# Attention scores whose low-part product uses 64 or 128 rows of the array, on one Trainium2 core

## The chip, the cores and the metric

The kernel runs on one core of a Trainium2 chip. The metric is the device time of one execution in microseconds (us); less is better. Engines are named as in the profile: PE is TensorE (matrix products), PEld its weight loads, DVE is VectorE, ACT is ScalarE, POOL is GpSimd, SP is the queue from which most transfers are issued.

## What is computed

One layer of a hybrid block: an input projection, a token mixer with two groups of eight heads (a matrix memory and a differential attention), an output projection and a gated feed-forward part. Batch 1, 512 latent and 256 context tokens, model width 2048. The change sits in the differential attention, which has two components of 64 channels per head:

```
s = jnp.einsum('bqhcd,bkhcd->bhcqk', qblk, k32) * scale
pr = jax.nn.softmax(s, axis=-1)
pd = pr[:, :, 0] - lam * pr[:, :, 1]
return jnp.einsum('bhqk,bkhe->bqhe', pd, v32)
```

Queries are the 512 latent tokens in blocks of 128, keys all 768 tokens. The scalar `lam` comes from four learned vectors of 64 numbers.

## The kernel before, in words

Matrix products run in a rounded 32-bit type. To keep accuracy, each operand is split into a high part (the rounded value, cast on ACT) and a low part (the rest, subtracted on DVE), and products of the parts are summed in PSUM. `load_w` (line 100) does this for every weight chunk of 128 x 512: `whi` on ACT (line 128), `wlo` on DVE (line 129). A projection (`proj`, line 433) multiplies the weights with 512 latent columns (tile `mm`, three products per contraction tile, `mm3`) and, for some outputs, with 256 context columns (tile `cx`).

**Startup.** `setup` loads the constant columns (`cols`, 522 wide, the last 256 of them the four vectors of `lam`) and tables; `startup` loads the 16 tiles `xT` of the input, takes their square sums, and computes the modulation (`mod`, from the chunks `mraw`) and the first projections.

**Attention.** From `attn_setup` on, TensorE runs in program order (`pin`). The projections of the heads go through, and after each short run of products `tick` (line 81) advances one of two queues of generators by one stage: even ticks those of the matrix memory (`mlstm_rest`), odd ticks those of the differential attention (`diff_rest`, line 763). So between two stages of `diff_rest` lie two runs of projection products and a stage of the other queue. The order on the other engines is a scheduler's, except that an engine runs its own list strictly in turn.

**A score.** `diff_q` (line 732) turns the queries of a head by the rotary tables and makes, per component, the tile `qa`: the high part of the 64 channels, twice over the 128 partitions; and one tile `ql` with the low parts of both components, 64 partitions each (line 744). `diff_k` makes per component `kb`: the high part of the keys on 64 partitions and the low part on the other 64. `score(t, c)` (line 769) then computes, for a query block t and a component c, 768 columns in two pieces of 512 and 256. Each piece is two products into the same PSUM columns: `qa` with all 128 rows of `kb` (high times high plus high times low), then `ql` with the 64 rows of the high keys:

```
for ks in (slice(0, 512), slice(512, TA)):
    self.mm(ps[:, ks], hd.qa[c][:, ts], hd.kb[c][:, ks], start=True, stop=False)
    self.mm(ps[:, ks], hd.ql[cs, ts], hd.kb[c][cs, ks], start=False, stop=True)
```

After the products DVE takes the row maximum (line 780, `mx<-sc`), scales it (line 781), and ACT takes the exponential (line 783, `p<-sc,mx`), which frees the PSUM tile `sc`. The pool of `sc` (`ps_big`) has one buffer, so the next score's products wait for that exponential. The stages of `diff_rest` are: score (0,0), transposed values (`vtp`), score (0,1), then for t = 1 to 3 score (t,0), `ptr` (transposes `pt`), score (t,1), `pv` (product `do`). Eight scores per head and eight heads make 64 scores.

Of the kernel before, what the change touches and what calls it, by code (L numbers as in the profile page):

```python
# [6 lines left out]
F32 = mybir.dt.float32  # L7
F32R = mybir.dt.float32r
AF = mybir.ActivationFunctionType
ALU = mybir.AluOpType  # L10
# [4 lines left out]
P = 128  # L15
# [17 lines left out]

# contraction groups of the output projection: the last heads come last
MIXG = [[0, 1, 2, 3], [8, 9, 10, 11], [4, 5, 12, 13], [6, 7, 14, 15]]
# [23 lines left out]
class Prog:  # L59
# [13 lines left out]
    def pe(self, ins):  # L73
        """in the pinned part TensorE runs in program order"""
        if self.pin:
            self.tc.keep_in_program_order(ins)
        return ins

    # one tick after every short run of projection products: the attention of earlier
    # heads goes between them, a stage at a time  # L80
    def tick(self):
# [18 lines left out]
    def load_w(self, src, n, act=False):  # L100
        """src [128, n] in DRAM -> get(column, width) -> (hi, lo)"""
        his, los = [], []
# [33 lines left out]

    # ---------------------------------------------------------------- setup
    def setup(self, ctx):
# [12 lines left out]
        self.dram = e(tc.tile_pool(name="scr", bufs=1, space=DRAM))  # L151
        self.cols = self.p_c.tile([P, NCOLS], F32, name="cols")
        self.tabs = self.p_c.tile([P, NTABS], F32, name="tabs")
        nc.sync.dma_start(self.cols, I["cols"])
        nc.sync.dma_start(self.tabs, I["tabs"])
# [13 lines left out]
    def rstd(self, dst, ss, n, scale):  # L169
        """dst = (ss*scale + eps) ** -0.5 for [128, n]"""  # L170
        nc = self.nc
        nc.vector.tensor_scalar(dst, ss, scale, EPS, ALU.mult, ALU.add)
        nc.gpsimd.tensor_tensor(dst, dst, self.mhalf[:, :n], ALU.pow)

    # ---------------------------------------------------------------- input norm statistics
    def rms_bcast(self, xs, w, name):
        """xs: 16 T-layout tiles [128, w]; returns rstd broadcast over partitions [128, w]"""
        nc = self.nc
# [25 lines left out]
    def mod_a(self, kt):  # L204
        """shift and scale columns of input channel tile kt, for latents and context"""
        nc, I = self.nc, self.I
# [27 lines left out]

    # ---------------------------------------------------------------- late modulation rows
    def modb_steps(self):
        """generator: one weight chunk per step; order ga1, sh2, sc2, ga2"""
        nc, I = self.nc, self.I
# [20 lines left out]
    def modb_cols(self, q, cc, acc):  # L259
        """columns of one of ga1 * g_post_mix, sh2, (1 + sc2) * g_pre_ffn, ga2 * g_post_ffn"""  # L260
        nc = self.nc
# [18 lines left out]

    # ---------------------------------------------------------------- combined input projection
    def phase_in(self):
# [7 lines left out]
        self.mcol = pc.tile([P, 64], F32, name="mcol")  # L290
        # lambda of the differential attention
        lam = self.C("lam").rearrange("p (a b) -> p a b", b=64)
        lt = self.slot("lt")[:, :128].rearrange("p (a b) -> p a b", b=64)
# [67 lines left out]
    def startup(self):  # L361
        nc, I = self.nc, self.I
        # silu of the conditioning vectors
        self.csil = self.p_st.tile([P, KT, 32], F32, name="csil", bufs=1)
# [86 lines left out]

    # ---------------------------------------------------------------- gates of the matrix memory
    def attn_setup(self):
# [22 lines left out]
    def gates(self):  # L476
# [4 lines left out]
        if True:  # L481
# [5 lines left out]
            for dst, r in ((I_, 0), (F_, 64)):  # L487
# [3 lines left out]
                nc.vector.tensor_copy(dst[32:40, TL:TA], gc[r + 32:r + 40, :])  # L491
            # log sigmoid
            nc.scalar.activation(L_, F_, AF.Abs)
            nc.scalar.activation(L_, L_, AF.Exp, scale=-1.0)
            nc.scalar.activation(L_, L_, AF.Ln, bias=1.0)
            nc.vector.scalar_tensor_tensor(F_, F_, 0.0, L_, ALU.min, ALU.subtract)
            # cumulative sums within chunks
            nc.vector.memset(L_, 1.0)
# [5 lines left out]
            nc.vector.tensor_tensor_scan(b_[32:40, ::-1], L_[32:40, ::-1], F_[32:40, ::-1], 0.0, ALU.mult, ALU.add)  # L504
            # running maxima carried over chunks
            nc.vector.tensor_tensor(I_, I_, b_, ALU.subtract)
# [31 lines left out]
            nc.scalar.activation(b_, b_, AF.Exp, scale=-1.0)  # L538
            # rows to be read back on all partitions
            self.row_d = self.dram.tile([2, 2, NH, TL], F32, name="row_d")  # L540
# [9 lines left out]
            for _ in range(9):  # L550
                yield
            # columns
            pa = self.p_at1
# [11 lines left out]

    # ---------------------------------------------------------------- matrix memory heads
    def conv3(self, dst, src, w, n):
# [29 lines left out]
    def tr6(self, src, name):  # L597
        """six 128 x 128 blocks of src [128, 768] transposed; two PSUM views [128, n, 128]"""
        out = []
        for a, n in ((0, 4), (4, 2)):  # L600
            ps = self.ps_sm.tile([P, 512], F32, tag="sm", name=name)
            for j in range(n):
                self.tr(ps[:, j * P:(j + 1) * P], src[:, (a + j) * P:(a + j + 1) * P], self.ident)
            out.append((a, n, ps[:, :n * P].rearrange("p (c d) -> p c d", d=P)))
        return out
# [18 lines left out]
    def mlstm_rest(self, hd, h):  # L624
# [9 lines left out]
        yield  # L634
        # weights within chunks, queries weighted for the carried states
        for d in range(2):
# [7 lines left out]
            nc.gpsimd.tensor_tensor(wrow[d], q, wrow[d], ALU.mult)  # L644
        # keys in natural layout, weighted for the state updates
        parts = self.tr6(k, "kt")
# [13 lines left out]
        yield  # L660
        # scores, shared by both directions
        pss = self.ps_sm.tile([P, 512], F32, tag="sm", name="s")
# [5 lines left out]
        yield  # L668
        # states before each latent chunk
        C = [self.p_cst.tile([P, 4, 129], F32, tag="cst", name="cst") for _ in range(2)]  # L670
# [51 lines left out]

    # ---------------------------------------------------------------- differential attention heads
    def rope(self, dst, src):
# [7 lines left out]
    def diff_q(self, hd, h):  # L732
        nc = self.nc
        q = self.acc.pop(DQ + h)
        self.rope(q, q)
        # per component the high part twice over the partitions, and the low parts
        hd.qa = [self.slot("qa", F32R) for _ in range(2)]
        hd.ql = self.slot("ql", F32R)
        for c in range(2):
            cs = slice(64 * c, 64 * c + 64)  # L740
            os = slice(64 - 64 * c, 128 - 64 * c)
            nc.scalar.copy(hd.qa[c][cs, :], q[cs, :])
            nc.scalar.copy(hd.qa[c][os, :], q[cs, :])
            nc.vector.tensor_tensor(hd.ql[cs, :], q[cs, :], hd.qa[c][cs, :].bitcast(F32), ALU.subtract)

    def diff_k(self, hd, h, psl, psc):
# [4 lines left out]
        self.rope(k[:, TC:TA], k[:, TC:TA])  # L751
        # per component high and low parts stacked over the partitions
        hd.kb = [self.p_a3.tile([P, 774], F32R, tag="a3", name="kb") for _ in range(2)]
# [9 lines left out]
    def diff_rest(self, hd, h):  # L763
        nc = self.nc
        on = self.slot("on")
        ss = self.p_s.tile([P, 4], F32, tag="oss", name="oss")
        st = {}

        def score(t, c):
# [3 lines left out]
            pr, z, mx = st[t]  # L773
            cs = slice(64 * c, 64 * c + 64)
            ts = slice(t * P, (t + 1) * P)
            ps = self.ps_big.tile([P, 1024], F32, tag="big", name="sc")
            for ks in (slice(0, 512), slice(512, TA)):
                self.mm(ps[:, ks], hd.qa[c][:, ts], hd.kb[c][:, ks], start=True, stop=False)
                self.mm(ps[:, ks], hd.ql[cs, ts], hd.kb[c][cs, ks], start=False, stop=True)
            nc.vector.reduce_max(mx[:, c:c + 1], ps[:, :TA], axis=AX.X)  # L780
# [19 lines left out]
        def pv(t):  # L800
# [6 lines left out]
            nc.scalar.activation(self.junk(), on[:, ts], AF.Square, accum_out=ss[:, t:t + 1])  # L807

        score(0, 0)
        yield  # L810
# [43 lines left out]

    # ---------------------------------------------------------------- products with activations stationary
    def nat_unit(self, get, acts, tt, y, cc, first, pool, tag):
# [13 lines left out]
    def nat_group(self, wsrc, acts, y, first, pool, tag):  # L870
        """y[tt][cc] += acts (4 contraction tiles) @ weights; wsrc(cc) is [128, 4*512]"""
        for cc in range(4):
# [112 lines left out]

    # ---------------------------------------------------------------- gated convolutional feed-forward
    def up_mm(self, m, t0, t1, part=None):
        """product m of the up projection for tokens t0..t1"""
        if part is None:
# [164 lines left out]
```

## Time and profile before

| | |
|---|---|
| median of 3 runs | 2825.64 us (2824.06 to 2826.68) |
| span of the profiled execution, first to last instruction | 2822.8 us |
| own time of the profiled execution | not given apart from its span; the three runs lie 1.3 to 3.9 us above that span |
| PE busy | 2763.3 us (98%), 13796 products |
| PEld busy | 2265.2 us (80%) |
| DVE busy | 1578.4 us (56%) |
| ACT busy | 1014.2 us (36%) |
| share of `sc` products in the chain that ended last | 3% |

How to read it: the span runs from the first instruction to the last. Busy time is the union of the times of an engine's instructions. Since products on PE overlap (the next starts while the one before drains), the cost of a product is read from the distance between the starts of one and the next, not from its duration. The chain that ended last is followed back from the last instruction, at each step to what released it.

### The profile page before, as it was taken

How to read it: one execution, taken by the hardware profiler on the slowest of the kernel's cores; microseconds unless marked ns; L12 is line 12 of the kernel's file. 1: busy time of each engine (PE TensorE's matmuls, PEld its weight loads, DVE VectorE, ACT ScalarE, POOL GpSimd, SP SyncE). 2: the span in 40 equal slices, each digit the busy share in tenths (PEclk: the TensorE clock that was granted, in tenths of full speed). 3: DMA queues.
4: the chain of work that ended last, by engine and by line, in shares of the span. 5: the costliest groups of instructions: out<-in, count | busy, mean ns of one | idle time of the engine just before them, and what ended most of it. 6: DMA issues, size and time to landing. Idle time of an engine off the chain costs nothing.

```text
span 2822.8 us, 35862 instructions
## 1 busy us (share of the span) xinstructions
PE 2763.3 (98%) x13796; PEld 2265.2 (80%) x13796; DVE 1578.4 (56%) x2826; ACT 1014.2 (36%) x1939; POOL 78.0 (3%) x101
## 2 busy tenths in 40 slices
PE   6999999999999999999899999999999999999998
PEld 3678788888888888887788888888888888888886
DVE  6585756665565655556634565544444444444446
ACT  4243334433433333534633232323232323323233
POOL 0000000000000000001000000000000000000000
PEclk9999999999999999999999999999999999999999
DMA  8865423433343434244223453532223232323234
GB/s 287 275 236 186 133 93 128 131 114 111 117 134 98 155 99 131 79 160 157 97 97 109 145 184 130 165 97 97 97 97 97 97 98 95 99 92 103 91 100 167
DMA packets 111818, 365.45 MB, mean 129 GB/s; under 512 B 12880, under 2 KB 13040, under 8 KB 111648
## 3 DMA queue, kind: packets, MB, share of 16 engines
q1 hardware_dynamic: 108000, 352.03, 37.8%
q0 software_dynamic: 3648, 11.14, 1.1%
q8 instruction: 108, 1.77, 0.3%
q14 instruction: 62, 0.51, 0.1%
HBM read 348.36 MB, written 14.76 MB: 129 GB/s over the span
## 4 chain that ended last, share of the span: by engine, by line
PE 80%; DVE 3%; DMA 2%; ACT 1%; issue 0%; POOL 0%; SPq 0%; POOLq 0%; DVEq 0%; ACTq 0%
PE mm L68 47%; PE nat L68 21%; PE cx L68 5%; PE sc L68 3%; PE do L68 1%; PE o L68 1%; DMA row<-row_d 1%; PE pt L71 1%; PE modr L68 0%; PE st L68 0%; PE vtp L71 0%; DMA raw<-in_wmB 0%; DVE xn L949 0%; ACT junk L892 0%; PE s L68 0%
## 5 line engine op out<-in xcount | busy, mean ns | idle before, releaser
L128 ACT CAST whi<-raw 128x512 fp32r<-128x512 f32 x792 | 489.5, 622 | 1155.5 <-PE mm L68 612.9
L129 DVE TENSOR_TENSOR wlo<-raw,whi 128x512 fp32r<-128x512 f32 x792 | 544.2, 691 | 616.7 <-ACT whi L128 610.2
L68 PE MATMUL mm<-hhi,whi 128*128 128x512 f32 (+1 forms) x1424 | 552.4, 388 | 3.8 <-DVE hhi L983 3.8
L68 PE MATMUL mm<-hhi,wlo 128*128 128x512 f32 (+1 forms) x1424 | 551.9, 388 | 0.8 <-DVE wlo L129 0.8
L68 PE MATMUL mm<-hlo,whi 128*128 128x512 f32 (+1 forms) x1424 | 552.0, 388 | 0.5 <-DVE hlo L984 0.3
L68 PE MATMUL mm<-lhi,whi 128*128 128x512 f32 x912 | 377.9, 415 | 1.5 <-ACT lhi L231 0.8
L68 PE MATMUL mm<-llo,whi 128*128 128x512 f32 x912 | 359.5, 394 | 0.3 <-DVE llo L233 0.3
L68 PE MATMUL mm<-lhi,wlo 128*128 128x512 f32 x912 | 359.6, 395 | 0.0
L68 PEld LDWEIGHTS mm<-hhi,whi 128*128 128x128 f32 x1424 | 268.1, 188 | 58.6 <-DVE hhi L983 4.2
L68 PEld LDWEIGHTS mm<-hhi,wlo 128*128 128x128 f32 x1424 | 268.1, 188 | 55.3 <-DVE wlo L129 1.0
L68 PEld LDWEIGHTS mm<-hlo,whi 128*128 128x128 f32 x1424 | 268.1, 188 | 54.6 <-DVE hlo L984 1.0
L68 PE MATMUL nat<-wlo,fhi 128*128 128x512 f32 x640 | 249.9, 390 | 0.0
L68 PE MATMUL nat<-whi,flo 128*128 128x512 f32 x640 | 249.9, 390 | 0.0
L68 PE MATMUL nat<-whi,fhi 128*128 128x512 f32 x640 | 248.9, 391 | 0.0
L868 DVE TENSOR_TENSOR y<-nat,y 128x512 f32<-128x512 f32 x208 | 141.9, 689 | 180.9 <-PE nat L68 180.7
L253 DVE SCALAR_TENSOR_TENSOR macc<-raw,c,macc 128x512 f32<-128x512 f32 x240 | 180.4, 752 | 94.1 <-DMA raw<-in_wmB 91.9
L68 PEld LDWEIGHTS mm<-lhi,whi 128*128 128x128 f32 x912 | 172.7, 189 | 42.5 <-issue 7.4
L68 PEld LDWEIGHTS mm<-lhi,wlo 128*128 128x128 f32 x912 | 171.7, 189 | 43.0 <-issue 3.7
L68 PE MATMUL cx<-chl,whi 128*128 128x256 f32 x1056 | 199.5, 287 | 0.5 <-DVE k L571 0.3
L68 PEld LDWEIGHTS mm<-llo,whi 128*128 128x128 f32 x912 | 173.2, 190 | 30.7 <-issue 2.9
L68 PEld LDWEIGHTS cx<-chl,whi 128*128 128x128 f32 x1056 | 168.7, 190 | 11.2 <-issue 1.6
L68 PE MATMUL cx<-chl,wlo 128*128 128x256 f32 x528 | 149.4, 283 | 0.0
(301 smaller groups left out, 3097.8 us busy)
## 6 DMA issues: line engine op xcount, KB each, us to landing
raw<-in_wu SPq DMA_DIRECT2D x176, 512.0 KB, 3.6
raw<-in_wmB SPq DMA_DIRECT2D x128, 512.0 KB, 3.9
raw<-in_w SPq DMA_DIRECT2D x105, 512.0 KB, 4.1
raw<-in_wd SPq DMA_DIRECT2D x88, 512.0 KB, 3.6
mraw<-in_wmA SPq DMA_DIRECT2D x64, 512.0 KB, 5.4
raw<-in_wo SPq DMA_DIRECT2D x32, 512.0 KB, 3.7
row<-row_d SPq DMA_DIRECT2D x32, 256.0 KB, 4.6
raw<-in_w SPq DMA_DIRECT2D x18, 256.0 KB, 4.3
```

Of the source, the lines that this page charges most:

```text
L68: return self.pe(self.nc.tensor.matmul(*a, **k))
L71: return self.pe(self.nc.tensor.transpose(out, in_, ident))
L128: self.nc.scalar.copy(hi, src)
L129: self.nc.vector.tensor_tensor(lo, src, hi.bitcast(F32), ALU.subtract)
L253: nc.vector.scalar_tensor_tensor(acc, r, c, acc, ALU.mult, ALU.add)
L868: nc.vector.tensor_tensor(y[tt][cc], ps, y[tt][cc], ALU.add)
```

## The change

`setup` loads the columns without the four vectors of `lam`, and `phase_in` loads those into a slot that is given back. `diff_q` makes no `ql` any more and keeps the turned queries (`hd.dq`). `diff_rest` gets a function `lows(t, c)`, which makes the low part of one query block and one component, 64 x 128, twice: once on its own 64 partitions and once on the other 64. `score` multiplies this 128-row tile with all 128 rows of `kb`, so that the low queries meet the high and the low keys. The lows of a score are asked for in the program right behind the products of the score before it; those of score (0,0) form a new first stage of the generator. The tiles `ql` come from a pool with 3 buffers. The change also drops comments and docstrings, so line numbers move.

```diff
@@ setup
-        self.cols = self.p_c.tile([P, NCOLS], F32, name="cols")
+        n = COLS["lam"][0]
+        self.cols = self.p_c.tile([P, n], F32, name="cols")
...
-        nc.sync.dma_start(self.cols, I["cols"])
+        nc.sync.dma_start(self.cols, I["cols"][:, :n])
@@ phase_in
-        lam = self.C("lam").rearrange("p (a b) -> p a b", b=64)
+        lam = self.slot("lam")[:, :256]
+        nc.sync.dma_start(lam, I["cols"][:, COLS["lam"][0]:])
+        lam = lam.rearrange("p (a b) -> p a b", b=64)
@@ diff_q
+        hd.dq = q
         hd.qa = [self.slot("qa", F32R) for _ in range(2)]
-        hd.ql = self.slot("ql", F32R)
...
-            nc.vector.tensor_tensor(hd.ql[cs, :], q[cs, :], hd.qa[c][cs, :].bitcast(F32), ALU.subtract)
@@ diff_rest
+        low = {}
+        def lows(t, c):
+            if t == 4:
+                return
+            cs = slice(64 * c, 64 * c + 64)
+            ts = slice(t * P, (t + 1) * P)
+            low[t, c] = self.p_s.tile([P, P], F32R, tag="ql", name="ql", bufs=3)
+            for to in (cs, slice(64 - 64 * c, 128 - 64 * c)):
+                nc.vector.tensor_tensor(low[t, c][to, :], hd.dq[cs, ts], hd.qa[c][cs, ts].bitcast(F32), ALU.subtract)
...
-            cs = slice(64 * c, 64 * c + 64)
             ts = slice(t * P, (t + 1) * P)
+            ql = low.pop((t, c))
...
                 self.mm(ps[:, ks], hd.qa[c][:, ts], hd.kb[c][:, ks], start=True, stop=False)
-                self.mm(ps[:, ks], hd.ql[cs, ts], hd.kb[c][cs, ks], start=False, stop=True)
+                self.mm(ps[:, ks], ql, hd.kb[c][:, ks], start=False, stop=True)
+            lows(t + c, 1 - c)
             nc.vector.reduce_max(mx[:, c:c + 1], ps[:, :TA], axis=AX.X)
...
+        lows(0, 0)
+        yield
         score(0, 0)
```

The new first stage moves the scores against the stages of the other queue. On PE, in the second head, this stood behind score (0,1) before (its last two products, then up to the second run of projection products; `ht` are transposes of the other queue):

```order
L68 MATMUL sc<-kb,qa 128x256
L68 MATMUL sc<-kb,ql 128x256
L68 MATMUL cx<-chl,whi 128x256 x2
L68 MATMUL cx<-chl,wlo 128x256
L68 MATMUL cx<-chl,whi 128x256 x2
L68 MATMUL cx<-chl,wlo 128x256
L68 MATMUL cx<-chl,whi 128x256 x2
L68 MATMUL cx<-chl,wlo 128x256
L68 MATMUL cx<-chl,whi 128x256 x2
L68 MATMUL cx<-chl,wlo 128x256
L71 MATMUL ht<-tabs,hn 128x128 x4
L68 MATMUL mm<-lhi,whi 128x512
```

And this stands behind the same score now, from its last two products on; two more such pairs of `cx` rows follow, and then score (1,0):

```order
L68 MATMUL sc<-kb,qa 128x256
L68 MATMUL sc<-kb,ql 128x256
L68 MATMUL mm<-lhi,whi 128x512
L68 MATMUL mm<-llo,whi 128x512
L68 MATMUL mm<-lhi,wlo 128x512
L68 MATMUL mm<-lhi,whi 128x512
L68 MATMUL mm<-llo,whi 128x512
L68 MATMUL mm<-lhi,wlo 128x512
L68 MATMUL cx<-chl,whi 128x256 x2
L68 MATMUL cx<-chl,wlo 128x256
L68 MATMUL cx<-chl,whi 128x256 x2
L68 MATMUL cx<-chl,wlo 128x256
```

The six `mm` and twelve `cx` products between the two scores are the same in number; the four transposes `ht` have left this gap for the one before score (0,1). That holds in heads 1 to 4; in the other heads no `ht` stood there.

On DVE, at the same two scores of the second head, this was the list from one row maximum to the next:

```order
L780 TENSOR_REDUCE mx<-sc 128x1
L781 TENSOR_SCALAR mx<-mx 128x1
L719 TENSOR_TENSOR acc<-ht,acc 128x512
L788 RECIPROCAL rz<-z 128x2
L129 TENSOR_TENSOR wlo<-raw,whi 128x512
L789 SCALAR_TENSOR_TENSOR cf<-rz,z,nlam 128x1
L790 SCALAR_TENSOR_TENSOR p<-p,cf 128x768
L780 TENSOR_REDUCE mx<-sc 128x1
```

This is the list now:

```order
L794 TENSOR_REDUCE mx<-sc 128x1
L780 TENSOR_TENSOR ql<-accr,qa 64x128
L795 TENSOR_SCALAR mx<-mx 128x1
L780 TENSOR_TENSOR ql<-accr,qa 64x128
L802 RECIPROCAL rz<-z 128x2
L803 SCALAR_TENSOR_TENSOR cf<-rz,z,nlam 128x1
L804 SCALAR_TENSOR_TENSOR p<-p,cf 128x768
L794 TENSOR_REDUCE mx<-sc 128x1
```

One low stands between the row maximum and its scaling, the other behind the scaling. Such a low is not that of the next score: the scheduler has put the lows two or three scores ahead of their use, as far as the three buffers let it. At 32 of the 64 row maxima a low stands in that place.

On SP's queue, this stood at the start of the program, behind the branch:

```order
L154 DMA cols<-in_cols 128x522
L155 DMA tabs<-in_tabs 128x514
L210 DMA mraw<-in_wmA 128x1024
L376 DMA xT<-in_xT 128x512 x16
L210 DMA mraw<-in_wmA 128x1024 x3
L109 DMA raw<-in_w 128x512
```

And this stands there now:

```order
L155 DMA cols<-in_cols 128x266
L156 DMA tabs<-in_tabs 128x514
L294 DMA lam<-in_cols 128x256
L211 DMA mraw<-in_wmA 128x1024 x2
L379 DMA xT<-in_xT 128x512 x16
L211 DMA mraw<-in_wmA 128x1024 x2
L109 DMA raw<-in_w 128x512
```

The vectors of `lam` have become a transfer of their own, and a second `mraw` chunk of 512 KB has moved ahead of the sixteen `xT` tiles.

## Rows read from the trace of the kernel before

**Rows 1.** The page: busy time of the engines, and the clock that TensorE was granted, in 40 slices of the span.

```profile
PE 2763.3 (98%) x13796; PEld 2265.2 (80%) x13796; DVE 1578.4 (56%) x2826; ACT 1014.2 (36%) x1939; POOL 78.0 (3%) x101
...
PEclk9999999999999999999999999999999999999999
```

**Rows 2.** The page: shares of the chain that ended last, by line.

```profile
PE mm L68 47%; PE nat L68 21%; PE cx L68 5%; PE sc L68 3%; PE do L68 1%; PE o L68 1%; DMA row<-row_d 1%; PE pt L71 1%; PE modr L68 0%; PE st L68 0%; PE vtp L71 0%; DMA raw<-in_wmB 0%; DVE xn L949 0%; ACT junk L892 0%; PE s L68 0%
```

**Rows 3.** Stretch of the 64 scores: busy PE, PEld, DVE, ACT, POOL; PEclk, DMA, GB/s.

```profile
300.00:1160.00 860.00, 848.24 (x4841) 710.20 (x4841) 525.24 (x1114) 341.08 (x746) 45.97 (x44) 1.00 0.38 121
```

**Rows 4.** Timeline of PE around one score: start us, duration us, rows*columns of the array.

```profile
708.58 0.39 PE L68 MATMUL mm<-lhi,wlo 128*128 128x512 f32 x1
708.81 0.40 PE L68 MATMUL sc<-kb,qa 128*128 128x512 f32 x1
709.13 0.50 PE L68 MATMUL sc<-kb,ql 64*128 64x512 f32 x1
709.56 0.39 PE L68 MATMUL sc<-kb,qa 128*128 128x256 f32 x1
709.88 0.38 PE L68 MATMUL sc<-kb,ql 64*128 64x256 f32 x1
710.19 0.50 PE L68 MATMUL mm<-lhi,whi 128*128 128x512 f32 x1
710.53 0.39 PE L68 MATMUL mm<-llo,whi 128*128 128x512 f32 x1
```

**Rows 5.** Timeline of PE behind another score, where 256-column products follow.

```profile
717.89 0.50 PE L68 MATMUL cx<-chl,whi 128*128 128x256 f32 x2
718.23 0.28 PE L68 MATMUL cx<-chl,wlo 128*128 128x256 f32 x1
718.35 0.40 PE L68 MATMUL cx<-chl,whi 128*128 128x256 f32 x2
```

**Rows 6.** Groups of PE in 300 to 1200 us: busy us, mean ns | idle before.

```profile
L68 PE MATMUL sc<-kb,ql 64*128 64x512 f32 x64 | 31.7, 495 | 0.0
...
L68 PE MATMUL sc<-kb,ql 64*128 64x256 f32 x64 | 24.4, 381 | 0.0
```

**Rows 7.** Waits of PE, 300 to 1200 us: us in total, times, longest.

```profile
PE sc L68 <- ACT p L783: 2.3, 2, 2.1
...
PE mm L68 <- ACT whi L128: 0.7, 1, 0.7
```

**Rows 8.** Waits over all engines in the same stretch: weight loads of the scores.

```profile
PEld sc L68 <- issue: 36.9, 128, 0.4
```

**Rows 9.** Groups of DVE in 300 to 1160 us, columns as in Rows 6.

```profile
L744 DVE TENSOR_TENSOR ql<-accr,qa 64x512 fp32r<-64x512 f32 x8 | 5.5, 684 | 2.4 <-PE sc L68 2.3
...
L655 DVE TENSOR_TENSOR kw<-kt,wscol 128x128 f32<-128x128 f32 x14 | 3.3, 278 | 0.0
```

**Rows 10.** Timeline of all engines from score (0,1) to score (1,0) of the sixth head.

```profile
850.32 0.50 PE L68 MATMUL cx<-chl,whi 128*128 128x256 f32 x2
850.43 0.96 DVE L780 TENSOR_REDUCE mx<-sc 128x1 f32<-128x768 f32 x1 [3.42 <-PE sc L68]
...
851.96 0.15 DVE L781 TENSOR_SCALAR mx<-mx 128x1 f32<-128x1 f32 x1
851.99 0.62 ACT L128 CAST whi<-raw 128x512 fp32r<-128x512 f32 x1 [4.94 <-PE cx L68]
...
852.51 0.90 ACT L783 ACTIVATE p<-sc,mx 128x768 f32<-128x768 f32 x1
...
852.75 0.68 DVE L129 TENSOR_TENSOR wlo<-raw,whi 128x512 fp32r<-128x512 f32 x1
...
853.01 0.39 PE L68 MATMUL mm<-lhi,wlo 128*128 128x512 f32 x1
...
853.55 0.51 PE L68 MATMUL sc<-kb,qa 128*128 128x512 f32 x1
```

**Rows 11.** Timeline of SP's queue at the start: time over which the transfers were issued.

```profile
2.12 11.17 SPq L376 DMA_DIRECT2D xT<-in_xT  x16
13.64 1.68 SPq L210 DMA_DIRECT2D mraw<-in_wmA  x3
```

## The prediction

> **What bounds the kernel now.** I read the page first, then the chain of waits, then the stretch in which the scores run, and last the distances between starts on TensorE. The page shows PE busy for 98% of the span at full granted clock, DVE at 56%, ACT at 36% [rows 1]. A busy PE is not yet a bound, so the chain comes next: it is made of PE lines, `mm` 47%, `nat` 21%, `cx` 5%, and `sc`, the scores, 3% [rows 2]. In the 860 us that hold the 64 scores PE is idle for 11.8 us, while DVE is busy 525 us and ACT 341 us [rows 3]. PE's waits there are few: 2.3 us in two scores that waited for the exponential before them, 0.7 us in one product that waited for a weight cast [rows 7]. So in this stretch the time is what PE's products take, one behind the other, and a product that becomes shorter takes its gain off the end, as long as the other engines stay ahead.
>
> What a product takes is the distance to the next start. In the timeline of a score the reader is to see that distances differ by the rows of the array [rows 4]. Ahead of the score, a 512-column product on 128 rows takes 0.23 us (708.58 to 708.81). Then `qa` on 128 rows, 0.32; `ql` on 64 rows, 0.43; `qa`, 256 columns, 0.32; `ql`, 0.31. Even the projection product behind the score takes 0.34 instead of 0.23. A 256-column product among products of 128 rows takes 0.12 us (718.23 to 718.35) [rows 5]. So each step from 128 rows to 64 or back costs 0.1 to 0.2 us beyond the streaming of columns. The weight loads say the same: those of the scores stood idle 36.9 us in 128 gaps for no wait that the profile shows [rows 8]. The score in the rows is a typical one: its 64-row products last 0.50 and 0.38 us [rows 4], the means over all 64 are 0.495 and 0.381 [rows 6]; and 64 scores at 1.38 us are 88 us, which is the 3% of the chain [rows 2].
>
> **The change part by part.**
>
> *The products of a score.* The number of products and columns stays; the two on 64 rows become products on 128. A score now takes 1.38 us from its first product to the next projection product, and that one 0.34, together 1.72 [rows 4]. With 128 rows everywhere I price a 512-column product at 0.23 and a 256-column one at 0.12: 0.23 + 0.23 + 0.12 + 0.12 = 0.70, and 0.23 for the product behind, together 0.93. The gain is 0.79 us per score. Where 256-column products follow, the first two take 0.34 [rows 5] instead of 0.24, so the gain is 0.78. 64 x 0.79 = 50.6 us, all on PE, all on the path. The trace has no score of four 128-row products; the bounds are 50.6 us, where they run as `mm` and `cx` do, and nothing, where the dear steps come from something that stays, such as a new weight tile for each product. I take the near end: `mm` products also get a new weight tile each, and take 0.23.
>
> A rule speaks against this. The Trainium skill, "TensorE: Matmul & The Clock Gate", section "Why this matters for your kernels", says that a product with a contraction of 32 takes as long as one of 128, and that a gain comes only from tiles running side by side. By that rule alone 64 and 128 rows cost the same, and this term would be zero. This trace disagrees for products that alternate between the two: 0.43 against 0.23 us.
>
> *The lows on DVE.* Removed are 16 subtractions of 64 x 512 at 0.684 us, 10.9 us; added are 8 scores x 2 halves x 8 heads = 128 of 64 x 128. The nearest row is a 128 x 128 `kw` at 0.278 [rows 9], so 35.6 us, and DVE has 24.7 us more to do. Its busy time in the stretch grows from 525 to 550 us while the stretch shrinks from 860 to about 812, from 61% to 68%. I cost this at nothing on the path: the lows read only `hd.dq` and `qa`, and the order has them two or three scores ahead of their use, so no product waits for one. What hides it is DVE's idle time; with that cover gone, it costs up to 24.7 us.
>
> *The wait for the one score buffer.* The order now puts a low between a row maximum and its scaling, so the exponential and the release of `sc` come up to 0.28 us later. That matters where two scores are close, at the eight steps from (0,1) to (1,0). At one of them [rows 10] the score's last product gives way at 850.32, the exponential ends at 853.41 (852.51 + 0.90) behind a weight cast of 0.62 us, and the next score starts at 853.55, though PE's last product before it was through at 853.24 (853.01 + 0.23): a wait of 0.31. After the change the chain is 3.23 + 0.28 = 3.51 us long and the products between take 2.82 (2.92 less the 0.10 of the dear first pair), a wait of 0.69. Two such waits are on record today [rows 7], so 2 x 0.38; the other six may come to 0.69, four of them because `ht` has left their gap. Upper end 0.8 + 4.1 = 4.9 us. Where no cast stands in the chain, it is 2.89 long and the wait is under 0.1, so the lower end is 0. Casts stand there in part of the heads; I take 2.0.
>
> *Startup.* One `mraw` chunk of 512 KB now goes ahead of the sixteen `xT`. These went out at 11.17 / 16 = 0.70 us per 256 KB [rows 11], so the last `xT` comes 1.4 us later. The square sums need all of them, and the first projection product needs the sums. The transfer of `lam` carries what `cols` has lost. Bounds 0 (the chunk would have come next anyway) and 1.8 (one more issue at 0.4); I take 1.4.
>
> *The moved stages.* Scores move by one stage of their queue; the odd ticks of a head, 24, still hold the 20 stages. At zero, within 3 us either way: a quarter of the 11.8 us in which PE stands idle there [rows 3].
>
> **Sum.** -50.6 + 2.0 + 1.4 = -47.2 us. Against the profiled span of 2822.8 that is 2775.6; the median of the runs, 2825.64, lies 2.8 above that span, and I expect the same distance: 2825.6 - 47.2 = **2778.4 us**.
>
> **The rivals.**
>
> *Waits take back a part.* If DVE and ACT run later as PE's work gets denser, each of the eight close steps waits for one more weight chunk, a cast and its subtraction, 0.62 + 0.68 = 1.30 us [rows 10]: 10.4 us in all, 2788.8. For it speaks that these steps already stand at the edge; against it, that the other 56 scores lie twice as many runs of products apart and that PE's waits are 3 us today [rows 7]. Chance 12%.
>
> *The change does not do what it says.* The dear steps come from something other than the rows, and stay; what is left is 2.0 + 1.4 of cost: 2829.0. Against it speak the 0.23 and 0.12 of all products around [rows 4, 5]. It is where the skill's rule above would lead. Chance 4%.
>
> *Slower: DVE's lows hold up the weights.* A low is queued ahead of `wlo`, and PE then waits for weights. The stretch has some 160 weight chunks; if each came late at PE by two lows, 0.56 us, that is 90 us, and the sum 2868. It decides only where a chunk is ready less than 0.56 us ahead of its use. The profile is against it: in the whole stretch PE waited once, 0.7 us, for a cast [rows 7]. Chance 2%.
>
> **How the numbers follow.** The forecast holds 82%: 2771 to 2785. The upper edge is the sum with the upper bounds of 4.9 and 1.8 and 3 us of moved stages; the lower is the full 50.6 with nothing given back, 3 us gained by the order, and 1 us for the spread of the runs. Since its edges are soft too, the range reaches on to the first rival and the same spread above it, so that less than 2 in 10 is outside: 2771 to 2791. About 0.2%, 5.7 us, is what a measurement of this kernel can tell from no change. Forecast and first rival are faster by more, 94%; the second rival lies within, 4%; the third is slower, 2%.
>
> **What would show it.** Right: in the changed profile all `sc` products read 128*128, their starts lie 0.23, 0.23, 0.12 and 0.12 us apart, the product behind follows after 0.23, the idle gaps of the scores' weight loads fall to almost nothing, and the chain's share of `sc` falls below 2%. The lows last about 0.28 us, 128 of them, and no PE wait names `ql`. PE's wait for `p` grows from 2.3 to about 4 us, and the first projection product comes 1 to 2 us later. Wrong: steps of 0.3 us or more between 128-row products (no gain), PE waits for `wlo`, `whi` or `p` of 10 us and more (waits in place of the steps), or a total below 2771, which would mean that the moved stages or products elsewhere have gained too.

## The result, and the profile after

The changed kernel takes **2776.16 us** (median of four runs, 2772.2 to 2777.48) against 2825.89 for the kernel before: 49.7 us less, a ratio of 0.9822 with a 95% interval of 0.9809 to 0.9836. The forecast was 2778.4 (2771 to 2791). Its profiled execution took 2775.6 us, with a span of 2773.8; the one before had a span of 2822.8, so 49.0 us are to be found between the two traces.

The page of the changed kernel: busy time of the engines, and the engines' shares of the chain that ended last.

```profile
PE 2714.9 (98%) x13796; PEld 2263.1 (82%) x13796; DVE 1603.4 (58%) x2938; ACT 1012.5 (37%) x1939; POOL 78.7 (3%) x101
...
PE 51%; DVE 2%; ACT 1%; issue 0%; DMA 0%; POOL 0%; POOLq 0%; DVEq 0%; ACTq 0%
```

PE did the same 13796 products in 48.4 us less [rows 1]; DVE has 25 us more. The chain is followed back over little more than half the span here (the shares add up to some 54%), and `sc` is not among the lines that the page names, so its share can't be compared with [rows 2].

A score in the timeline of PE after the change, columns as in [rows 4]:

```profile
684.80 0.28 PE L68 MATMUL cx<-chl,wlo 128*128 128x256 f32 x1
684.92 0.40 PE L68 MATMUL sc<-kb,qa 128*128 128x512 f32 x1
685.15 0.40 PE L68 MATMUL sc<-kb,ql 128*128 128x512 f32 x1
685.39 0.28 PE L68 MATMUL sc<-kb,qa 128*128 128x256 f32 x1
685.51 0.28 PE L68 MATMUL sc<-kb,ql 128*128 128x256 f32 x1
685.63 0.39 PE L68 MATMUL mm<-lhi,whi 128*128 128x512 f32 x1
685.86 0.40 PE L68 MATMUL mm<-llo,whi 128*128 128x512 f32 x1
```

The products lie 0.23, 0.24, 0.12 and 0.12 us apart, and the one behind takes 0.23: 0.94 us where it was 1.72 [rows 4]. The idle time of the scores' weight loads that no wait explained, 36.9 us [rows 8], is gone from the list of waits of 300 to 1160 us; what is left of it there is the wait for the score buffer:

```profile
PEld sc L68 <- ACT p L797: 10.7, 5, 4.0
```

Where did the time go, stage by stage? The context products `cx` begin with the first projection of the attention and end with the last, in every version. Their group in the trace (min/median/max duration, then the first and the last start) marks off the stage (the last one or two of the 64 scores come behind it); first the kernel before, then the changed one:

```profile
L68 PE MATMUL cx<-chl,whi x1056: 276/283/390, 249.9 to 1151.3; 128*128 128x256 f32 x176
```

```profile
L68 PE MATMUL cx<-chl,whi x1056: 274/283/562, 252.7 to 1105.6; 128*128 128x256 f32 x176
```

The startup is 2.8 us longer, the attention fell from 901.4 to 852.9 us, 48.5 less, and what follows it from 1671.5 to 1668.2. I do not put the last 3.3 us down to the change: this part took 1667.2 to 1671.5 us in the twelve traces, and about 2 us of the difference go with the clock, whose mean in the 52 us at the end (2770 to 2822) was 0.93 before, and 0.97 in the corresponding 53 us (2720 to 2773).

The scores are priced as forecast, and yet the attention gained a little less than 50.6 us. The waits of PE after the change, us in total, times, longest, tell of more:

```profile
PE sc L68 <- ACT p L797: 9.7, 5, 3.8
...
PE pt L71 <- DVE mx L795: 2.3, 1, 2.3
...
PE o L68 <- DVE cst L689: 0.2, 1, 0.2
```

The wait for the one score buffer has grown from 2.3 us [rows 7] to 9.7, and another wait, that of the products `o` for the carried states `cst`, has nearly gone. Before the change it was the largest of the list:

```profile
PE o L68 <- DVE cst L686: 5.5, 4, 2.7
```

The prediction had named the first and not the second. The experiments are about these two.

### The profile page after: what moved, and what is told of

It is laid out like the page before. It is cut to its first block, busy times and chain, and to the rows that moved or that the text cites. A ratio compares the mean times of both kernels' runs of the same rounds, so it can differ in the third digit from the quotient of the medians.

```text
span 2773.8 us, 35993 instructions
## 1 busy us (share of the span) xinstructions
PE 2714.9 (98%) x13796; PEld 2263.1 (82%) x13796; DVE 1603.4 (58%) x2938; ACT 1012.5 (37%) x1939; POOL 78.7 (3%) x101
## 4 chain that ended last, share of the span: by engine, by line
PE 51%; DVE 2%; ACT 1%; issue 0%; DMA 0%; POOL 0%; POOLq 0%; DVEq 0%; ACTq 0%
PE mm L68 34%; PE nat L68 16%; ACT junk L908 0%; DVE x L1038 0%; DVE y L884 0%; DVE y L1030 0%; DVE xn L965 0%; DMA raw<-in_wd 0%; POOL rs L174 0%; ACT hf L996 0%; DVE hlo L1000 0%; DVE wact L129 0%; DVE y L955 0%; PE modr L68 0%; ACT y L972 0%
```

## The experiments

The attention's length is read from the group of `cx` as above, in the one execution of each version that was traced (for "changed, no stage" that is the slowest of its five, 2781.2 us); medians are of all runs, and ratios are against the kernel before, run on the same chip.

| version | low product | new stage | median us | ratio, 95% interval | attention us |
|---|---|---|---|---|---|
| before | 64 rows | no | 2824.7 to 2825.9 | | 901.4 |
| lows per block (and the transfer of lam), 64 rows | 64 rows | no | 2821.15 | 0.9989 (0.9980 to 0.9997) | 898.8 |
| stage alone | 64 rows | yes | 2813.73 | 0.9967 (0.9956 to 0.9978) | 889.1 |
| changed, back to 64 rows | 64 rows | yes | 2811.07 | 0.9955 (0.9939 to 0.9972) | 885.5 |
| before, products grouped | 64 rows | no | 2803.64 | 0.9927 (0.9912 to 0.9942) | 882.2 |
| lows of a whole head | 128 rows | no | 2784.02 | 0.9856 (0.9841 to 0.9871) | 863.6 |
| changed, no stage | 128 rows | no | 2775.79 | 0.9827 (0.9814 to 0.9840) | 858.7 |
| changed | 128 rows | yes | 2776.16 | 0.9822 (0.9809 to 0.9836) | 852.9 |
| changed, lam late | 128 rows | yes | 2770.53 | 0.9811 (0.9797 to 0.9826) | 852.6 |
| changed, gap | 128 rows | moved | 2764.06 | 0.9785 (0.9771 to 0.9798) | 843.5 |
| whole head, gap, lam late | 128 rows | moved | 2763.26 | 0.9782 (0.9767 to 0.9797) | 841.8 |
| gap and lam late | 128 rows | moved | **2760.73** | 0.9773 (0.9759 to 0.9786) | 840.7 |

### The rows alone, undone

```diff
-                self.mm(ps[:, ks], ql, hd.kb[c][:, ks], start=False, stop=True)
+                self.mm(ps[:, ks], ql[64 * c:64 * c + 64, :], hd.kb[c][64 * c:64 * c + 64, ks], start=False, stop=True)
```

> The changed kernel, with the low product of each score taken back to 64 rows (its own half of the low tile with the high keys); the lows per block, the new stage and the transfer of lam stay as changed. If the array rows are the cause, the steps of 0.32, 0.43, 0.32, 0.31 us come back, a score takes 1.38 us and delays the product behind by 0.11, 64 x 0.79 = 50 us are lost less up to 7 us of waits for the score buffer that the longer scores hide: 2819 to 2827 us. If the gain came from anything else in the change (lows nearer to their use, the moved stages, the freed slots), the time stays at 2772 to 2780.

Measured: 2811.07 us. A score of this version in the timeline of PE:

```profile
601.06 0.40 PE L68 MATMUL sc<-kb,qa 128*128 128x512 f32 x1
601.39 0.49 PE L68 MATMUL sc<-kb,ql 64*128 64x512 f32 x1
601.81 0.38 PE L68 MATMUL sc<-kb,qa 128*128 128x256 f32 x1
602.13 0.38 PE L68 MATMUL sc<-kb,ql 64*128 64x256 f32 x1
602.44 0.50 PE L68 MATMUL mm<-lhi,whi 128*128 128x512 f32 x1
602.77 0.40 PE L68 MATMUL mm<-llo,whi 128*128 128x512 f32 x1
```

The dear steps are back to a hundredth, 1.38 and 0.33 us for 1.38 and 0.34, with everything else of the change in place: the rows are their cause. But the time lies between the two expectations. Only 34.9 us were lost, and the version is 14 us faster than the kernel before with the same scores. Its waits say where:

```profile
PE sc L68 <- ACT p L797: 1.4, 1, 1.4
...
PE o L68 <- DVE cst L689: 0.3, 1, 0.3
```

The score buffer is waited for less than in either kernel, and the states hardly any more. So something in the change beside the rows seems to gain, and shorter scores to lose a part of it again. Two candidates: the moved stage, and the lows made per block.

### The moved stage alone, and the lows per block alone

The first is the kernel before with one line more, the second the changed kernel with 64 rows and without its first stage.

```diff
+        yield
         score(0, 0)
         yield
```

> The kernel before with nothing but one empty stage ahead of score (0,0), so that the scores stand one stage later against the other queue, as in the changed kernel; the low products keep their 64 rows. The run with 64 rows inside the changed kernel was 14 us faster than the kernel before though its scores took as long, and PE waited 2.9 us for others in the attention where the kernel before waits 11.5. If the moved stage is the reason, this one too is 12 to 18 us faster, 2808 to 2814 us, and o's wait for cst (5.5 us before) is gone. If the lows made per block are the reason, it stays at 2822 to 2828.

```diff
         lows(0, 0)
-        yield
         score(0, 0)
...
-                self.mm(ps[:, ks], ql, hd.kb[c][:, ks], start=False, stop=True)
+                self.mm(ps[:, ks], ql[64 * c:64 * c + 64, :], hd.kb[c][64 * c:64 * c + 64, ks], start=False, stop=True)
```

> The complement: the changed kernel with 64-row low products and without the new first stage, so that of the change only the lows per block and the transfer of lam are left. If the moved stage is what gained, nothing is gained here: 2822 to 2830 us, o waits for cst about 5 us. If the lows per block gained, 2808 to 2816 us.

Measured: 2813.73 us for the stage alone, 11.0 less than before and inside the range expected; 2821.15 for the lows and the transfer of lam without the stage, 3.6 less, a little under the range expected. PE's waits with the stage alone:

```profile
PE sc L68 <- ACT p L783: 3.4, 3, 2.7
...
PE o L68 <- DVE cst L686: 0.4, 1, 0.4
```

and without the stage:

```profile
PE o L68 <- DVE cst L689: 5.9, 5, 2.7
PE sc L68 <- ACT p L797: 2.6, 1, 2.6
```

An empty stage, with no product and no low in it, takes most of the 14 us. It puts the scores one stage later against the matrix memory, and the products `o` then find their states ready. In the list of PE's waits the total falls from 11.5 to 5.2 us. Behind two of the waits for the states the clock had been lower before, with a mean of 0.83 from 390 to 400 us and of 0.79 from 693 to 701; with the stage there is one such stretch (0.83 from 320 to 330), behind a wait for the score buffer. By these clocks about 1.7 us more come back. The attention is 12.3 us shorter, of which 1.7 us are one score that now stands behind the last `cx`. What the remaining 2.6 us are, no run shows.

### The stage taken out of the changed kernel

```diff
         lows(0, 0)
-        yield
         score(0, 0)
```

> The changed kernel without the new first stage: the lows of score (0,0) are asked for in the stage of that score. The transposes ht stand again between scores (0,1) and (1,0) in heads 1 to 4. Theory of the moved stage: it took 5.3 us of waits for the carried states away (o waits for cst: 5.5 us before, 0.2 after) and gave about 7 us of waits for the score buffer (2.3 before, 9.7 after); undone, the waits swap back, buffer 3 to 6 us, states about 5, and the time is within 3 us of the changed kernel. Theory of the lows: they alone lengthen the wait for the buffer, it stays at 9 to 10 us, the states' wait comes on top, and the time is 2779 to 2783.

Measured: 2775.79 us, the same as the changed kernel within the runs' spread (2774.3 to 2781.2).

```profile
PE o L68 <- DVE cst L689: 5.5, 5, 2.8
PE cx L68 <- DVE k L574: 3.1, 4, 1.7
PE sc L68 <- ACT p L797: 2.6, 2, 2.4
```

As the theory of the moved stage expected, the waits swap back. With the runs above this makes a square. The rows are worth 45.4 us without the stage (2821.15 to 2775.79) and 34.9 with it (2811.07 to 2776.16). The stage is worth 10 to 11 us with 64 rows and nothing that shows with 128 in the medians, though the two traced executions differ by 5.6 us. In the changed kernel the two overlap.

### The products in another order

```diff
             for ks in (slice(0, 512), slice(512, TA)):
                 self.mm(ps[:, ks], hd.qa[c][:, ts], hd.kb[c][:, ks], start=True, stop=False)
+            for ks in (slice(0, 512), slice(512, TA)):
                 self.mm(ps[:, ks], hd.ql[cs, ts], hd.kb[c][cs, ks], start=False, stop=True)
```

> The kernel before, with the four products of a score in another order: both 128-row products first, then both 64-row ones, so that the array goes from 128 to 64 rows and back once per score, not twice. If a step between row counts is what costs, the products lie 0.23, about 0.3, 0.23, 0.31 us apart with 0.34 behind, 1.41 for 1.72: 64 x 0.31 = 20 us are gained, 2800 to 2812 us. If a 64-row product is slow by itself, both still cost what they did and the time stays at 2822 to 2830.

Measured: 2803.64 us, 21 less than before and inside the range expected, with nothing changed but the order. A score, two products to a row:

```profile
714.70 0.52 PE L68 MATMUL sc<-kb,qa 128*128 128x512 f32 x2
715.15 0.62 PE L68 MATMUL sc<-kb,ql 64*128 64x512 f32 x2
715.69 0.50 PE L68 MATMUL mm<-lhi,whi 128*128 128x512 f32 x1
716.03 0.40 PE L68 MATMUL mm<-llo,whi 128*128 128x512 f32 x1
```

From the first `qa` to the first `ql` it is 0.45 us where two such products take 0.35, and the two `ql` take 0.54. With the product behind, 0.34, that is 1.33 us, against 1.72 with four changes of row count and 0.94 with none. So each change costs about 0.2 us, and a 64-row product is not slow for itself. The Trainium skill, "TensorEngine Tiling (Array Packing)", section "Key Properties", says that changing the tiling mode, not just the tile, drains TensorE; the three orders agree, 0.2 us for each change of row count, though no row shows the drain itself. It is this rule that fits the runs, and not the one on the contraction length weighed in the prediction.

### The low parts by another way

```diff
+        hd.ql = [self.slot("ql", F32R) for _ in range(2)]
...
+            for to in (cs, os):
+                nc.vector.tensor_tensor(hd.ql[c][to, :], q[cs, :], hd.qa[c][cs, :].bitcast(F32), ALU.subtract)
...
-                self.mm(ps[:, ks], ql, hd.kb[c][:, ks], start=False, stop=True)
+                self.mm(ps[:, ks], hd.ql[c][:, ts], hd.kb[c][:, ks], start=False, stop=True)
...
-        lows(0, 0)
-        yield
         score(0, 0)
```

> The 128-row product by another way: diff_q makes the low part of a whole head once per component, 64 x 512 on both halves (32 subtractions in place of 128 small ones), and the scores read blocks of it; no lows between row maximum and scaling, and no new first stage. (One more slot of 512 columns, and the small row tile of the modulation moved into a slot.) If the rows are the cause, each score takes 0.70 us here too, and the wait for the score buffer is 2 to 6 us, because ht stands again in the gap of heads 1 to 4: 2768 to 2777 us. If the low made close to its use matters, it stays nearer to 2826.

Measured: 2784.02 us, 40.9 less than before and 7 outside what was expected. The wait for the score buffer was 1.8 us, at the low end, but others grew; three of PE's waits:

```profile
PE o L68 <- DVE cst L689: 5.1, 5, 2.7
PE pt L71 <- DVE kw L658: 4.6, 5, 1.5
PE mm L68 <- DVE wlo L129: 4.4, 1, 4.4
```

The last one is one wait in the first head. While PE waited (to 297.68), DVE's list held, ahead of the weight chunk, the work on the gates:

```profile
294.01 0.94 DVE L535 TENSOR_TENSOR g_l<-g_i,g_ml 40x768 f32<-40x768 f32 x1
294.88 0.94 DVE L540 TENSOR_TENSOR g_b<-g_b,g_m 40x768 f32<-40x768 f32 x1
...
296.94 0.69 DVE L129 TENSOR_TENSOR wlo<-raw,whi 128x512 fp32r<-128x512 f32 x1
```

That is near the third rival's mechanism, a weight chunk late behind other DVE work, at one place; but the work ahead of it is that of the gates, and not a low. Whether the lows in one piece per head, or the slots that moved with them, push the list into this order was not tried apart.

### The score buffer, and lam

The gap puts the extra stage between scores (0,1) and (1,0):

```diff
         lows(0, 0)
-        yield
         score(0, 0)
...
         score(0, 1)
         yield
+        yield
         for t in range(1, 4):
```

> The changed kernel with its extra stage put between scores (0,1) and (1,0) in place of ahead of score (0,0), so that four runs of projection products stand between these two and not two. If the single score buffer holds up the close steps, PE's wait for p falls from 9.7 us to under 1, the clock dip that follows the longest of these waits goes too, and 8 to 12 us come off against the same kernel without the gap: 2764 to 2769 us. If DVE's list is what is late, the wait moves to other lines (pt, o, the later scores) and the time is 2772 to 2778.

The other edit moves the load of lam, and the five instructions on it, from the start of `phase_in` into `attn_setup`:

> The changed kernel, with lam loaded and its exponentials taken only when the attention starts. The list of SP then begins with the sixteen xT ahead of all mraw chunks. If the transfer of lam and the second mraw chunk ahead of xT are what delayed the startup (first projection product at 33.0 us for 32.0, first context product at 252.7 for 249.9), 1 to 4 us come back: 2772 to 2775 us. If the delay is the scheduler's order of the first products, nothing comes back: 2776 plus or minus 1.5.

> The gap between scores (0,1) and (1,0), and lam loaded late, together. If the two are independent, their gains add: 2760 to 2767 us. If the later start is taken up by the attention anyway, it is no faster than the gap alone.

> Lows of a whole head made once on both halves, the gap between scores (0,1) and (1,0), and lam loaded late. Against the version with lows per block DVE has 64 x 512 subtractions, 32 x 0.68 = 22 us in place of 36, and none stands between row maximum and scaling. If that delay still costs, 1 to 3 us less than with lows per block; if the gap hides it, the same within 1.5 us.

Measured: 2764.06 us with the gap, 12.1 less than the changed kernel and at the lower edge of the range; 2770.53 with lam late, 5.6 less, where 1 to 4 were expected; 2760.73 with both, inside its range, so the gains add but for some 2 us. PE's waits with the gap:

```profile
PE cx L68 <- DVE k L574: 4.9, 4, 2.0
PE sc L68 <- ACT p L797: 1.9, 3, 0.8
```

The wait for the buffer fell from 9.7 to 1.9 us, not under 1, and a new one of 4.9 us stands first. With lam late, the transfers at the start of SP's queue are these:

```profile
1.65 9.17 SPq L368 DMA_DIRECT2D xT<-in_xT  x16
11.16 2.36 SPq L211 DMA_DIRECT2D mraw<-in_wmA  x4
```

The sixteen `xT` are out at 10.8 us where they took to 13.3 [rows 11] before and to 14.75 in the changed kernel. The first projection product starts at 30.33 us (31.97 before, 33.02 in the changed kernel), and the attention at 248.3. The whole-head lows with both edits gave 2763.26 (2759.4 to 2768.7), 2.5 more than the lows per block, and outside both expectations; the same single wait of 4.4 us for `wlo` is in its trace. Lows made per block are no worse in these runs, then, though DVE does more.

## Why the prediction was right, and where it was not

The total was right, -47.2 forecast and -49.7 measured. It was right by its largest term, and by luck in two others, whose errors cancelled: some 14 us given back where 2.0 were priced, and 12.3 gained in the attention where nothing was.

- **Products of a score, -50.6 us: right in size and place.** 0.94 us was measured in the score shown for the 0.93 priced. What the rule of the Trainium skill that the prediction weighed ("TensorE: Matmul & The Clock Gate", section "Why this matters for your kernels") would have meant, no gain, did not happen; with the rows undone the steps came back. What a score gives back on PE is not all seen at the end, though: 35 to 45 us by the square of runs.
- **Lows on DVE, nothing on the path: right.** The group of the lows of four heads in the changed kernel:

```profile
L780 DVE TENSOR_TENSOR ql<-accr,qa x64: 259/286/1342, 350.6 to 720.4; 64x128 fp32r<-64x128 f32 x64
```

   The median is 0.286 us for the 0.28 taken, DVE's busy time grew by 25.0 us for the 24.7 reckoned, and no wait of PE names `ql`.
- **The wait for the score buffer, +2.0 us: too small.** PE's waits there rose by 7.4 us, above the upper end of 4.9. The step that failed is the chain: I added the low's 0.28 us to an exponential that stood behind a weight cast, and took DVE to be on time. The longest wait, in the fifth head, shows what else can stand there. DVE after score (0,1), whose products end at 693.0:

```profile
692.90 0.69 DVE L129 TENSOR_TENSOR wlo<-raw,whi 128x512 fp32r<-128x512 f32 x1 [0.71 <-ACT whi L128]
695.98 1.54 DVE L254 SCALAR_TENSOR_TENSOR macc<-raw,c,macc 128x512 f32<-128x512 f32 x2 [2.39 <-DMA raw<-in_wmB]
697.44 0.95 DVE L794 TENSOR_REDUCE mx<-sc 128x1 f32<-128x768 f32 x1
...
698.50 0.14 DVE L795 TENSOR_SCALAR mx<-mx 128x1 f32<-128x1 f32 x1
```

   The row maximum had to wait in DVE's list behind a modulation step that itself waited 2.39 us for a transfer. PE's timeline:

```profile
695.67 0.28 PE L68 MATMUL cx<-chl,wlo 128*128 128x256 f32 x1
699.78 0.80 PE L68 MATMUL sc<-kb,qa 128*128 128x512 f32 x1 [3.83 <-ACT p L797]
700.38 0.63 PE L68 MATMUL sc<-kb,ql 128*128 128x512 f32 x1
...
701.66 0.63 PE L68 MATMUL mm<-llo,whi 128*128 128x512 f32 x1
702.08 0.63 PE L68 MATMUL mm<-lhi,wlo 128*128 128x512 f32 x1
```

   PE stood still for 3.83 us, and behind that the products of 512 columns take 0.42 us in place of 0.23: the clock had fallen to its lower level, a mean of 0.62 from 697 to 706 us and 0.50, the 1.2 GHz level, from 699 to 704. The price of the wait did not include this.

   The rows of before could have told of it. The two waits on record there were 2.1 and 0.2 us [rows 7], and not twice the 0.31 us of the sixth head that I took as the pattern. The long one stood in the first head, behind the same step of DVE's list:

```profile
313.49 1.54 DVE L253 SCALAR_TENSOR_TENSOR macc<-raw,c,macc 128x512 f32<-128x512 f32 x2 [1.89 <-DMA raw<-in_wmB]
314.94 0.95 DVE L780 TENSOR_REDUCE mx<-sc 128x1 f32<-128x768 f32 x1
```

   In the changed kernel the three longest waits for the buffer (3.8, 2.4 and 2.0 us of the 9.7) and the 2.3 us of `pt` stand behind such a step that waited for its transfer.
- **The moved stages, 0 within 3 us: the term that failed.** An empty stage alone gains 11.0 us, 12.3 in the attention. My working said only that the 20 stages still fit into 24 ticks. It did not ask which waits between the two queues the old places caused, although 5.5 us of `o` waiting for `cst` stood in the list of waits that I read, above the rows that I used. So "PE's waits are 3 us today" was a wrong reading: the whole list came to 11.5.
- **Startup, +1.4 us: right in direction.** The first projection product came 1.05 us later, the first context product 2.8. Loading lam late brought back 4.4 in the trace: with the last `xT` issued 1.5 us later than before in the changed kernel and 2.5 us earlier with lam late, the first projection product moved the same way, 1.05 later and 1.6 earlier. So the order of the transfers is the likely cause; the five instructions on lam moved with them and were not tried apart.

The attention can be added up from this. The products give 50.6 us and the stage 12.3, 62.9 in all; 48.5 were measured, so 14.4 went back. The two traces with the same stage, stage alone and changed, show where. Both have 62 scores ahead of the last `cx`, 62 x 0.79 = 49.0 us, and the attention is 36.2 shorter, so 12.8 went back there. PE's listed waits rose from 5.2 us to some 13, which is 7.8. The lower clock cost about 1.7 us with the stage alone (0.83 from 320 to 330) and about 5.7 in the changed kernel (0.76 from 320 to 327 and from 604 to 611, 0.50 from 699 to 704 and 0.91 from 704 to 708), an estimate from these clocks and the time that PE was busy in them, so 4.0 more. That makes 11.8 of the 12.8. That the shorter scores themselves brought these waits out is what the square shows.

The first rival, waits that take back a part, thus did happen, in about the size priced (14 us given back for its 10) but by another way: not a weight chunk at each of the eight close steps, but four long waits behind transfers and the lower clock after three of them. A gain that I had not priced paid for it.

## What to carry to other kernels

Read the price of a product from the distance between starts, and look at products that change the number of array rows: each change cost 0.2 us here, so that a product with twice the needed rows, or merely a grouped order, was the faster one. When a hand-made interleaving moves by a stage, price the waits that the old places caused, in both directions; they are in the list of waits by name. And after a bound engine gets faster, look where two steps share one buffer and stand close: 12 us more lay in one stage of distance.

## What the runs showed of the hardware

The price of a change of row count falls on two steps, about half on the one that leads up to the first product of the new count and half on the one behind it, and it is the same in both directions: 0.09 to 0.11 us each time. In the grouped order the two 64-row products take 0.54 us together, 0.35 as two of 128 rows do and 0.19 for the two halves of the price that fall on them, so nothing is left that 64 rows would cost for themselves.

A wait of PE of 3.83 us was followed by products at half speed, at a granted clock of 0.50 from 699 to 704 us. In the kernel before, waits of 2.7 and 1.6 us for the states were followed by stretches with a mean of 0.83 and 0.79. In the changed kernel taken back to 64 rows PE's longest wait in the attention is 1.4 us, ahead of a score at 713 us, and the mean from 710 to 720 us was 1.00.
